# A three-branch decoder layer on one core: late loads behind casts, a split first cast, half of the cross scaling on GpSimd, and new places for the side work

## Chip, cores and metric

The kernel runs on one core of a Trainium2 chip. The time is device microseconds of one execution. The unchanged kernel takes 323.5 us (median of three runs, 323.2 to 323.61). The rows below come from one profiled execution that took 324.77 us, 1.27 us more than that median. TensorE was granted its upper level of 2.4 GHz throughout (mean granted clock 0.999 of full speed).

## What is computed

One decoder layer for 256 tokens of width 1024 in fp32. All shapes are those of the code; `rmsnorm`, `rope` and the two attentions' softmax are the usual ones.

```python
h = rmsnorm(x, g_in)
z = h @ w_in                                    # 1024 x 8776
(mq, mk, mv, mg, dq, dk, dv, dg, iq, ik, iw, xq, xg, glog) = jnp.split(z, offs, axis=-1)
ya = moba_attention(rope(mq), rope(mk), mv)     # 8 heads of 64, causal, one block of 256
ya = (ya * silu(mg)) @ w_up_moba
yb = dsa_attention(rope(dq), rope(dk), dv, rope(iq), rope(ik), iw)   # causal, top 64 keys
yb = (yb * silu(dg)) @ w_up_dsa
kv = rmsnorm(mem, g_mem) @ w_mem_kv             # 256 memory rows
xk, xv = kv[..., :512], kv[..., 512:]
yc = cross_attention(xq, xk, xv)                # 4 heads of 128
yc = (yc * silu(xg)) @ w_up_cross
gates = sigmoid(glog + b_merge)                 # 3 branches x 1024
u = gates[0] * ya + gates[1] * yb + gates[2] * yc
out = rmsnorm(x + u @ w_out, g_final)
```

## The kernel before

**Products.** An fp32 product is made of three matmuls in the type fp32r. Each operand is split into a high half (a cast to fp32r) and a low half (the operand minus its high half); high times high, high times low and low times high are added up in PSUM. The weights come from HBM in 100 pieces of up to 512 KB, called steps (w0, w1, ...). For each step the program loads the piece into a raw buffer (`load_weights`; four raw buffers, tag `wraw`), splits it (`split_weights`: ScalarE, ACT in the profile, writes the high half `w3h`, VectorE, DVE, the low half `w3l`), and TensorE multiplies. Loads are called six steps ahead (`LOAD_AHEAD`), the split three steps ahead (`SPLIT_AHEAD`). The pieces of steps 0 to 3 are cast in two parts. The first eight steps belong to mv and mq in turn (mv, mq, mv, mq, ...); then `ORDER` lists the blocks: `i0`, `dq0` and so on are column blocks of `w_in`, `xk0`, `xk1`, `xv` of `w_mem_kv`, `l10` is a block of the gate logits (branch 1, columns 256 times 0), `u00` a block of an up projection.

**Side work.** Everything else is hung on a step or half a step with `at(step, fn, ...)`, and the places stand in tables by hand: `M_PAIRS` and `D_PAIRS` (scores, transposes and values of the two self attentions), `X_HEADS` (the four cross heads: scores at h0, scaling at h0 + 0.5, transposes at h0 + 2, values at h0 + 3.5), `TURNS` (rope), `IDX` (the index heads of the sparse attention), `GATES` (silu), `MEM` (the four loads of the memory rows and their statistics). What a `w_in` block leaves in PSUM is evacuated at its end; for a logit block, `logit_evac` multiplies on DVE and then takes a Sigmoid on ACT.

**Order.** TensorE (PE) and GpSimd (POOL) run in the order of the program text. The rows of ACT, DVE and SyncE (SP), which issues most loads, are ordered by a scheduler, so a new place can move their rows as well. PE waits where an operand's half has not been written yet, or where a PSUM bank has not been read yet.

**The start.** The loads of x's first block and of steps 0 to 2 are issued on SP. `load_late` is called behind the cast of step 0: it issues step 3's weights and x's third pair of blocks on ACT (behind the last cast of w0), and steps 4 and 5 and x's last pair on SP. x in rows (`x_rows`, 1 MB, from which the norm is taken) is issued at step -2, and read by `xjunk` on ACT.

**The cross scaling.** In `cross_scale` DVE takes the reciprocal of the row sums (`xst`), and then ACT scales both halves of the head's probabilities (`xpr`, two of 128x256). The transposes (`xpt`) on PE read both. `self_scale` does the same for the self attentions, with both parts on POOL.

## Time and profile before

| | before |
|---|---|
| median of three runs | 323.5 us (323.2 to 323.61) |
| the profiled execution | 324.77 us |
| its span in the trace | 323.0 us |
| PE busy | 313.0 us (97%) |
| DVE busy | 252.1 us (78%) |
| ACT busy | 202.9 us (63%) |
| POOL busy | 41.9 us (13%) |
| chain that ended last | PE 70%, DVE 15%, DMA 5%, ACT 4%, issue 4% |

The span is the time from the first to the last instruction in the trace; the execution's own time has 1.77 us around it. The chain is followed back from the last instruction to whatever released each step of it. Rows of waits name the instruction that waited, what released it, and for how long.

### The profile page before, as it was taken

Reading aid. Unit: us, or ns where it says so; the run is one execution under the profiler, and the core shown is the slowest. Engines: PE = TensorE matmul, PEld = TensorE weight load, DVE = VectorE, ACT = ScalarE, POOL = GpSimd, SP = SyncE. Lnnn points to the kernel's source line nnn. Section 1 sums busy time; section 2 is a strip of 40 time slices with the busy share of each in tenths; the row PEclk is TensorE's granted clock in tenths of the full one; section 3 lists DMA queues with packets and bytes.
Section 4 is the critical chain, followed back from the end, with each engine's and each line's share of the span. In section 5 each row is a group of like instructions: output and inputs, shape, how many; then the busy total and the mean of one; then the engine's idle time right before and its main releaser. Section 6 shows DMA issues by size and latency. Waiting matters only on the chain.

```text
span 323.0 us, 6395 instructions
## 1 busy us (share of the span) xinstructions
PE 313.0 (97%) x2442; PEld 297.4 (92%) x2442; DVE 252.1 (78%) x458; ACT 202.9 (63%) x357; POOL 41.9 (13%) x58
## 2 busy tenths in 40 slices
PE   8899999998999999999999999999999999999992
PEld 7699999988999989879999999999999999998882
DVE  3579999899799999988766759998466775677523
ACT  5599674687878545577666588756444546643434
POOL 0001000017202000010200235321000111014011
PEclk9999999999999999999999999999999999999999
DMA  6989886864644446574443434478765666655003
GB/s 202 379 293 333 269 269 194 265 240 124 214 130 127 138 130 210 182 246 131 146 132 117 146 94 162 136 220 302 211 193 189 190 188 205 182 156 188 2 0 130
DMA packets 18368, 59.45 MB, mean 184 GB/s; under 512 B 2209, under 2 KB 2465, under 8 KB 18337
## 3 DMA queue, kind: packets, MB, share of 16 engines
q1 hardware_dynamic: 17760, 57.73, 57.1%
q10 hardware_dynamic: 576, 1.31, 1.0%
q8 instruction: 19, 0.31, 0.5%
q14 instruction: 13, 0.10, 0.1%
HBM read 55.89 MB, written 1.05 MB: 176 GB/s over the span
## 4 chain that ended last, share of the span: by engine, by line
PE 70%; DVE 15%; DMA 5%; ACT 4%; issue 4%; SPq 0%; ACTq 0%; DVEq 0%
DMA w3r<-w_in 3%; DVE wk L498 2%; DMA w25r<-w_in 2%; DVE m L496 1%; PE o_0ps L255 1%; PE o_0ps L256 1%; PE o_0ps L254 1%; DMA w0r<-w_in 1%; PE dya L642 1%; PE i_0ps L280 1%; PE i_1ps L280 1%; PE mv_1ps L280 1%; PE mv_0ps L280 1%; DVE acc L487 1%; PE lg L480 1%
## 5 line engine op out<-in xcount | busy, mean ns | idle before, releaser
L747 POOL TENSOR_TENSOR u<-u,gt 128x512 f32<-128x512 f32 x7 | 9.9, 1411 | 76.7 <-DVE gt L744 76.7
L616 POOL TENSOR_SCALAR dpr<-dpr,dst 128x128 f32<-128x128 f32 (+1 forms) x16 | 6.6, 425 | 84.1 <-DVE dst L614 83.9
L616 POOL TENSOR_SCALAR mpr<-mpr,mst 128x128 f32<-128x128 f32 (+1 forms) x16 | 9.8, 629 | 56.3 <-DVE mst L614 56.3
L734 ACT ACTIVATE gt<-gt,x_first 128x256 f32<-128x256 f32 x24 | 10.9, 501 | 2.7 <-DVE gt L731 2.5
L606 ACT ACTIVATE dpr<-dms,dst 128x128 f32<-128x128 f32 (+1 forms) x16 | 7.1, 446 | 3.6 <-DVE dst L602 3.6
L788 ACT ACTIVATE junk<-xn 128x512 f32<-128x512 f32 (+1 forms) x5 | 2.7, 543 | 8.6 <-DVE xn L786 8.6
L606 ACT ACTIVATE mpr<-mms,mst 128x128 f32<-128x128 f32 (+1 forms) x16 | 7.1, 444 | 1.2 <-DVE mst L602 1.2
L664 ACT ACTIVATE xpr<-xsc,xst,xs_rstd 128x256 f32<-128x256 f32 x8 | 4.4, 560 | 3.4 <-DVE xst L660 3.4
L752 ACT CAST us<-u 128x512 fp32r<-128x512 f32 x4 | 2.5, 624 | 6.2 <-POOL u L747 4.9
L647 ACT COPY dyT<-dya 64x256 f32<-64x256 f32 x8 | 2.9, 367 | 4.2 <-PE dya L642 4.1
L484 ACT ACTIVATE rl<-lg 128x384 f32<-128x384 f32 x8 | 3.9, 485 | 2.7 <-PE lg L480 1.6
L487 DVE SCALAR_TENSOR_TENSOR acc<-rl,iw,acc 128x128 f32<-128x128 f32 (+1 forms) x14 | 5.4, 431 | 0.1
L480 PE MATMUL lg<-ikT,iqT 128*128 128x128 f32 (+1 forms) x32 | 5.1, 282 | 0.1
L968 PE MATMUL warm<-ones 128*128 128x128 f32 x18 | 4.0, 419 | 1.1 <-DVE eps_t L963 1.1
L602 DVE CUSTOM_DVE_ANT_0 mms<-msc,bias_c 128x128 f32<-128x128 f32 (+1 forms) x16 | 5.0, 350 | 0.0
L968 PEld LDWEIGHTS warm<-ones 128*128 128x128 f32 x18 | 3.9, 328 | 1.1 <-DVE eps_t L963 1.1
L648 DVE TENSOR_TENSOR dyT<-dyT,dya 64x256 f32<-64x256 f32 x8 | 3.3, 417 | 1.8 <-ACT dyT L647 1.7
L628 ACT CAST dph<-dtp 128x384 fp32r<-128x384 f32 x8 | 3.8, 479 | 1.4 <-PE dtp L627 1.3
L629 DVE TENSOR_TENSOR dpl<-dtp,dph 128x384 fp32r<-128x384 f32 x8 | 4.4, 553 | 0.4
L602 DVE CUSTOM_DVE_ANT_0 dms<-dsc,sel 128x128 f32<-128x128 f32 (+1 forms) x16 | 4.7, 352 | 0.0
L786 DVE TENSOR_TENSOR xn<-o_0ps,xn 128x512 f32<-128x512 f32 x2 | 1.4, 691 | 4.2 <-PE o_0ps L256 4.2
L498 DVE MATCH_REPLACE8 wk<-m,wk 128x128 f32<-128x128 f32 (+1 forms) x14 | 4.7, 342 | 0.0
(1296 smaller groups left out, 1541.9 us busy)
## 6 DMA issues: line engine op xcount, KB each, us to landing
x_rows<-x SPq DMA_DIRECT2D x2, 512.0 KB, 8.7
eT<-memT SPq DMA_DIRECT2D x4, 256.0 KB, 4.6
xn<-x SPq DMA_DIRECT2D x2, 512.0 KB, 5.5
w0r<-w_in SPq DMA_DIRECT2D x2, 256.0 KB, 3.3
w1r<-w_in SPq DMA_DIRECT2D x2, 256.0 KB, 4.9
xT<-xT SPq DMA_DIRECT2D x2, 256.0 KB, 7.1
w2r<-w_in SPq DMA_DIRECT2D x1, 512.0 KB, 7.3
w3r<-w_in ACTq DMA_DIRECT2D x1, 512.0 KB, 8.7
```

The source lines that it names most:

```text
L280: nc.tensor.matmul(accs[nm][t][:, :n], a[p](k, slice(t * P, (t + 1) * P)), w[q][:, half, :], start=k + i == 0, stop=k + i == nk + 1,)
L480: nc.tensor.matmul(lg[:, c : c + n], q[:, q0:q1], idx["k"][:, j, 0:n], start=j == 0, stop=j == 1)
L487: nc.vector.scalar_tensor_tensor(acc[:, c], rl[:, c], iw[:, t, g : g + 1], (bias_c if g == 0 else acc)[:, c], op0=OP.mult, op1=OP.add,)
L498: nc.vector.match_replace(out=wk[:, c], in_to_replace=m8[t], in_values=src[:, c], imm_value=TAKEN)
L602: nc.vector.tensor_tensor_reduce(out=ms[:, c], in0=sc[:, c], in1=bias()[:, c], op0=OP.add, op1=OP.min, scale=-(HD**-0.5), scalar=3e38, acc ...
L606: big["last_exp"] = nc.scalar.activation(pr[:, c], ms[:, c], AF.Exp, bias=st[:, t : t + 1], scale=-1.0, accum_out=st[:, 2 + t : 3 + t],)
L616: nc.gpsimd.tensor_scalar(pr[:, c], pr[:, c], st[:, 4 + t : 5 + t], 1.0, op0=OP.mult, op1=OP.mult)
L629: nc.vector.tensor_sub(pl, tp[:, 0 : 3 * P], ph.bitcast(F32))
L664: big["last_exp"] = nc.scalar.activation(pr3[:, t, :], sc[:, t, :], AF.Exp, bias=st[:, t : t + 1], scale=xs_rstd[:, t : t + 1], accum_out= ...
L734: nc.scalar.activation(gt[:, f, :], gt[:, f, :], AF.Sigmoid, bias=x_first[:, j : j + 1])
L747: adder.tensor_tensor(u, u, gt, op=OP.add)
L968: nc.tensor.matmul(warm[:, 0:P], ones, ones, start=True, stop=True)
```

## The change

The order of the loads changes. x's third pair and step 3's weights are issued on ACT behind the first part of w1's cast (before: behind w0's cast), step 4's weights on ACT behind its second part (before: on SP); step 5's weights come before x's last pair on SP. `LOAD_ROWS` goes from -2 to 1, so `x_rows` is issued behind step 6's weights, and the constants behind `x_rows`. The first cast (128x512 of w0) is split by columns: ACT casts one half and DVE the other. In `cross_scale` POOL scales the second half of each head's probabilities. `ORDER` puts `xk1` ahead of `dv`, `l10` ahead of `dg0` (before: behind `xg1`), and changes the order of the last logit and up blocks; the place tables have new numbers.

```diff
@@ -62,24 +62,24 @@
 WARM = 9
 HALVED = 2
 ORDER = (
-    "mk0", "mk1", "i0", "dq0", "xq0", "i1", "dq1", "dk0", "dk1", "xk0", "xq1", "dv", "xk1",
-    "xv", "mg0", "mg1", "dg0", "dg1", "xg0", "xg1", "l10", "l01", "l00", "u00", "l02", "u10",
-    "l20", "l03", "u01", "u02", "l21", "u03", "u20", "l11", "u11", "l22", "l23", "u21", "l12",
+    "mk0", "mk1", "i0", "dq0", "xq0", "i1", "dq1", "dk0", "dk1", "xk0", "xq1", "xk1", "dv",
+    "xv", "mg0", "mg1", "l10", "dg0", "dg1", "xg0", "xg1", "l00", "u00", "l01", "l02", "u01",
+    "u10", "l03", "l20", "l21", "u20", "l11", "l23", "u03", "l22", "u11", "u02", "u21", "l12",
     "l13", "u12", "u13", "u23", "u22",
 )
-LOAD_ROWS = -2
+LOAD_ROWS = 1
 X_STATS = 6
 
-IDX = (27, 29, 33.5)
-
-TURNS = (('mq', 8.5, 15.5), ('mk', 13.5, 20.5), ('dq', 27, 30), ('dk', 34, 37.5))
-
-M_PAIRS = ((23, 25.5), (24, 27.5), (26.5, 29.5), (29.5, 31.5))
-D_PAIRS = ((43.5, 47.5), (47.5, 49), (52, 53.5), (54.5, 55.5))
-X_HEADS = (41.5, 44.5, 49, 50.5)
-GATES = 59.5
-
-MEM = (2, 7, 11, 15, 21.5)
+IDX = (27, 29, 34)
+
+TURNS = (('mq', 8.5, 15), ('mk', 14.5, 20.5), ('dq', 27, 33.5), ('dk', 36, 39))
+
+M_PAIRS = ((23, 25.5), (24.5, 27.5), (26.5, 29.5), (29.5, 31.5))
+D_PAIRS = ((43.5, 47.5), (47, 49), (52, 53.5), (54.5, 55.5))
+X_HEADS = (41.5, 44.5, 49, 50)
+GATES = 57.5
+
+MEM = (3, 7.5, 10.5, 13, 22)
 
 
 def block_places(blocks, nk):
@@ -224,7 +224,7 @@
 
 
     loaded, halves = {}, {}
-    last_hi = [None]
+    last_hi, last_load = [None], [None]
 
     def load_weights(s, j=None, queue=nc.sync):
         src, off, nk_all, n, k0, nk = plan.steps[s][0]
@@ -235,7 +235,9 @@
             tensor=src.tensor, offset=src.offset + off + (k0 + a) * n,
             ap=[[nk_all * n, P], [1, (b - a) * n]],
         )
-        queue.dma_start(loaded[s][:, a:b, :].rearrange("p k n -> p (k n)"), v)
+        last_load[0] = queue.dma_start(
+            loaded[s][:, a:b, :].rearrange("p k n -> p (k n)"), v
+        ).ins
 
     def split_weights(s):
         raw = loaded.pop(s)
@@ -245,7 +247,13 @@
         part = 1 if s < HALVED + 2 else shape[1]
         for j in range(0, shape[1], part):
             ks = slice(j, j + part)
-            last_hi[0] = nc.scalar.copy(hi[:, ks, :], raw[:, ks, :]).ins
+            cols = slice(0, shape[2] // 2 if s + j == 0 else shape[2])
+            last_hi[0] = nc.scalar.copy(hi[:, ks, cols], raw[:, ks, cols]).ins
+            if s + j == 0:
+                cols = slice(shape[2] // 2, shape[2])
+                nc.vector.tensor_copy(hi[:, ks, cols], raw[:, ks, cols])
+            if s == 1:
+                load_late(j)
             nc.vector.tensor_sub(lo[:, ks, :], raw[:, ks, :], hi[:, ks, :].bitcast(F32))
         halves[s] = (hi, lo)
 
@@ -609,13 +617,14 @@
                 )
             prs[nm, hd] = (pr, st)
 
+    def pool_scale(r, factor):
+        nc.gpsimd.tensor_scalar(r, r, factor, 1.0, op0=OP.mult, op1=OP.mult)
+
     def self_scale(nm, hd):
         pr, st = prs[nm, hd]
         nc.vector.reciprocal(st[:, 4:6], st[:, 2:4])
         for t, c in PARTS:
-            nc.gpsimd.tensor_scalar(
-                pr[:, c], pr[:, c], st[:, 4 + t : 5 + t], 1.0, op0=OP.mult, op1=OP.mult
-            )
+            pool_scale(pr[:, c], st[:, 4 + t : 5 + t])
 
     def self_transpose(nm, hd):
         pr, _ = prs.pop((nm, hd))
@@ -670,10 +679,8 @@
     def cross_scale(hd):
         pr, st = prs["x", hd]
         nc.vector.reciprocal(st[:, 4:6], st[:, 2:4])
-        for t in range(2):
-            nc.scalar.activation(
-                pr[:, t, :], pr[:, t, :], AF.Copy, scale=st[:, 4 + t : 5 + t]
-            )
+        nc.scalar.activation(pr[:, 0, :], pr[:, 0, :], AF.Copy, scale=st[:, 4:5])
+        pool_scale(pr[:, 1, :], st[:, 5:6])
 
     def cross_transpose(hd):
         pr, _ = prs["x", hd]
@@ -882,13 +889,14 @@
     attend("m", M_PAIRS, lambda: bias_c)
     attend("d", D_PAIRS, lambda: idx["sel"])
 
-    x_rows = []
+    x_rows, rows_load = [], [None]
 
     def load_rows():
         for t in range(2):
             rows = keep.tile([P, 4, S], F32, name=f"x_rows{t}", tag=("khi", "klo")[t])
             rows = rows.rearrange("p a b -> p (a b)")
-            nc.sync.dma_start(rows, x[t * P : (t + 1) * P, :])
+            with tc.issue_after(last_load[0]):
+                rows_load[0] = nc.sync.dma_start(rows, x[t * P : (t + 1) * P, :]).ins
             x_rows.append(rows)
 
     def start_stats():
@@ -959,6 +967,7 @@
     at(end["u01"], load_tail)
 
 
+    first = [load_act(xT, 0, "x", 0)]
     nc.vector.memset(ones, 1.0)
     nc.vector.memset(eps_t, EPS)
     nc.scalar.copy(ss[:, 3:4], eps_t)
@@ -966,36 +975,37 @@
     warm = psum.tile([P, 512], F32, name="warm", tag="tp", bufs=1)
     for _ in range(WARM):
         nc.tensor.matmul(warm[:, 0:P], ones, ones, start=True, stop=True)
-    first = [load_act(xT, 0, "x", 0)]
     load_weights(1, 0)
     load_weights(1, 1)
     first.append(load_act(xT, 0, "x", 1))
     load_weights(2)
 
-    def load_late():
+    def load_late(j):
 
         with tc.issue_after(last_hi[0]):
-            load_weights(3, queue=nc.scalar)
-            first.append(load_act(xT, 0, "x", 2, nc.scalar))
-        load_weights(4)
-        load_weights(5)
-        first.append(load_act(xT, 0, "x", 3))
+            if j == 0:
+                first.append(load_act(xT, 0, "x", 2, nc.scalar))
+                load_weights(3, queue=nc.scalar)
+            else:
+                load_weights(4, queue=nc.scalar)
+                load_weights(5)
+                with tc.issue_after(last_load[0]):
+                    first.append(load_act(xT, 0, "x", 3))
 
     for s in range(-SPLIT_AHEAD, n):
         p, rest = divmod(s + SPLIT_AHEAD, 2)
         if p < 4 and not rest:
             first[p]()
         if s == 4:
-            nc.sync.dma_start(cst, consts[:, 0:512])
-            nc.sync.dma_start(tabT.rearrange("p t c -> p (t c)"), consts[:, 512:1024])
+            with tc.issue_after(rows_load[0]):
+                nc.sync.dma_start(cst, consts[:, 0:512])
+                nc.sync.dma_start(tabT.rearrange("p t c -> p (t c)"), consts[:, 512:1024])
         for fn, args in plan.side.pop(s, []):
             fn(*args)
         if LOAD_AHEAD <= s + LOAD_AHEAD < n:
             load_weights(s + LOAD_AHEAD)
         if s + SPLIT_AHEAD < n:
             split_weights(s + SPLIT_AHEAD)
-            if s + SPLIT_AHEAD == 0:
-                load_late()
         if s >= 0:
             w = halves.pop(s)
             plan.steps[s][1](w, 0)
```

How rows move. First ACT, at the start of the program: the casts of w0 to w2 (`w0h`, ...), the casts of x's blocks (`xhi`) and the loads that ACT issues. Before:

```order
L248 CAST w0h<-w0r 128x512
L185 ACTIVATE xhi<-xT,x_first 128x256
L248 CAST w0h<-w0r 128x512
L177 DMA xT<-xT 128x512
L238 DMA w3r<-w_in 128x1024
L248 CAST w1h<-w1r 128x512 x2
L185 ACTIVATE xhi<-xT,x_first 128x256 x2
L248 CAST w2h<-w2r 128x512 x2
```

Now:

```order
L251 CAST w0h<-w0r 128x256
L185 ACTIVATE xhi<-xT,x_first 128x256
L251 CAST w0h<-w0r 128x512
L251 CAST w1h<-w1r 128x512
L177 DMA xT<-xT 128x512
L238 DMA w3r<-w_in 128x1024
L251 CAST w1h<-w1r 128x512
L238 DMA w4r<-w_in 128x1024
L185 ACTIVATE xhi<-xT,x_first 128x256 x2
L251 CAST w2h<-w2r 128x512 x2
```

The two loads stand one cast later, and a third one, w4's, has come in between the second cast of w1 and x's cast.

Second DVE, around step 20, where it evacuates the first cross query block (`xqT`) and turns the keys of the first attention (`mkT`). Before:

```order
L249 TENSOR_TENSOR w22l<-w22r,w22h 128x640
L249 TENSOR_TENSOR w23l<-w23r,w23h 128x640
L562 TENSOR_TENSOR xqT<-xq0ps,xqT 128x512
L532 TENSOR_TENSOR mkT<-mkT,mksw 128x1024
L249 TENSOR_TENSOR w24l<-w24r,w24h 128x1024
```

Now:

```order
L257 TENSOR_TENSOR w22l<-w22r,w22h 128x640
L570 TENSOR_TENSOR xqT<-xq0ps,xqT 128x512
L257 TENSOR_TENSOR w23l<-w23r,w23h 128x640
L540 TENSOR_TENSOR mkT<-mkT,mksw 128x1024
L257 TENSOR_TENSOR w24l<-w24r,w24h 128x1024
```

The subtraction of step 23's weights has moved from ahead of `xqT` to behind it.

Third ACT, at steps 50 to 52, between the transposes of the sparse attention (`dph`) and the next cast of its probabilities (`dpr`), where the last cross head is handled (`xpr`). Before:

```order
L628 CAST dph_2296<-dtp_2298 128x384
L664 ACTIVATE xpr_2335,xst_2332<-xsc_2325,xst_2332,xs_rstd 128x256 x2
L248 CAST w55h<-w55r 128x1024
L647 COPY dyT<-dya_2289 64x256
L688 CAST xph_2361<-xpt_2356 128x512
L674 ACTIVATE xpr_2335<-xpr_2335,xst_2332 128x256 x2
L248 CAST w56h<-w56r 128x1024
L606 ACTIVATE dpr_2414,dst_2413<-dms_2412,dst_2413 128x128
```

Now:

```order
L637 CAST dph_2297<-dtp_2299 128x384
L741 ACT_TABLE_LOAD
L741 ACTIVATE gt_2318<-gt_2318,x_first 128x256 x2
L673 ACT_TABLE_LOAD
L673 ACTIVATE xpr_2315,xst_2312<-xsc_2305,xst_2312,xs_rstd 128x256 x2
L656 COPY dyT<-dya_2290 64x256
L695 CAST xph_2367<-xpt_2362 128x512
L682 ACTIVATE xpr_2315<-xpr_2315,xst_2312 128x256
L251 CAST w55h<-w55r 128x1024
L251 CAST w56h<-w56r 128x1024
L695 CAST xph_2434<-xpt_2429 128x512
L614 ACTIVATE dpr_2417,dst_2416<-dms_2415,dst_2416 128x128
```

The two Sigmoids of `l10` (`gt`) now stand between two groups of exponentials, each time with a load of ACT's function table ahead of the next function, and `xpr` is scaled once here instead of twice.

## Rows read from the trace of the kernel before

**Rows 1.** The page's chain that ended last, by engine.

```profile
PE 70%; DVE 15%; DMA 5%; ACT 4%; issue 4%; SPq 0%; ACTq 0%; DVEq 0%
```

**Rows 2.** PE timeline, first matmuls of steps 2, 4 and 6; columns: start us, us, engine, line.

```profile
11.99 0.50 PE L280 MATMUL mv_0ps<-w2h,xhi 128*128 128x512 f32 x1 [0.34 <-ACT w2h L248]
...
18.86 0.40 PE L280 MATMUL mv_0ps<-w4h,xhi 128*128 128x512 f32 x1
...
24.45 0.40 PE L280 MATMUL mv_0ps<-w6h,xhi 128*128 128x512 f32 x1
```

**Rows 3.** ACT timeline at the start; in brackets the idle time before and its releaser.

```profile
5.62 0.39 ACTq L177 DMA_DIRECT2D xT<-xT  x1
6.05 1.31 ACTq L238 DMA_DIRECT2D w3r<-w_in  x1
7.41 0.62 ACT L248 CAST w1h<-w1r 128x512 fp32r<-128x512 f32 x1 [1.17 <-DMA w1r<-w_in]
8.57 0.62 ACT L248 CAST w1h<-w1r 128x512 fp32r<-128x512 f32 x1 [0.54 <-DMA w1r<-w_in]
9.83 0.91 ACT L185 ACTIVATE xhi<-xT,x_first 128x256 fp32r<-128x256 f32 x2 [0.64 <-DMA xT<-xT]
11.32 1.14 ACT L248 CAST w2h<-w2r 128x512 fp32r<-128x512 f32 x2 [0.58 <-DMA w2r<-w_in]
14.76 1.14 ACT L248 CAST w3h<-w3r 128x512 fp32r<-128x512 f32 x2 [2.30 <-DMA w3r<-w_in]
```

**Rows 4.** What the DMA engines moved in 0 to 25 us, 40 slices.

```profile
GB/s 0 0 23 234 242 288 311 256 285 229 292 236 246 252 311 262 374 390 416 410 403 416 420 429 413 426 419 420 419 367 380 321 157 177 167 49 292 331 308 387
```

**Rows 5.** PE's weight-load waits, 22 to 200 us: total, times, longest.

```profile
PEld mya L642 <- DVE mpl L629: 1.2, 1, 1.2
PEld xpt L684 <- ACT xpr L674: 0.7, 2, 0.5
```

**Rows 6.** DVE timeline, 57 to 64 us.

```profile
57.94 0.81 DVE L249 TENSOR_TENSOR w23l<-w23r,w23h 128x640 fp32r<-128x640 f32 x1
59.33 0.69 DVE L562 TENSOR_TENSOR xqT<-xq0ps,xqT 128x512 fp32r<-128x512 f32 x1 [0.58 <-ACT xqT L561]
...
63.81 0.17 DVE L219 RECIPROCAL m_rstd<-en 128x2 f32<-128x2 f32 x1 [0.32 <-ACT en L218]
```

**Rows 7.** DVE and POOL timeline, 76 to 78 us, and POOL's scalings by form, 140 to 200 us.

```profile
76.33 1.20 DVE L249 TENSOR_TENSOR w29l<-w29r,w29h 128x1024 fp32r<-128x1024 f32 x1
76.41 1.47 POOL L616 TENSOR_SCALAR mpr<-mpr,mst 128x256 f32<-128x256 f32 x1
...
L616 POOL TENSOR_SCALAR dpr<-dpr,dst 128x256 f32<-128x256 f32 x8 | 3.8, 479 | 0.0
```

**Rows 8.** Timeline of all engines at the first cross head's scaling.

```profile
140.91 0.16 DVE L672 RECIPROCAL xst<-xst 128x2 f32<-128x2 f32 x1
...
140.99 1.23 DVE L249 TENSOR_TENSOR w47l<-w47r,w47h 128x1024 fp32r<-128x1024 f32 x1
...
141.10 0.91 ACT L674 ACTIVATE xpr<-xpr,xst 128x256 f32<-128x256 f32 x2
```

**Rows 9.** Timeline of all engines, 171 to 182 us.

```profile
171.64 0.56 ACT L664 ACTIVATE xpr<-xsc,xst,xs_rstd 128x256 f32<-128x256 f32 x1 [1.48 <-DVE xst L660]
...
176.55 1.23 DVE L249 TENSOR_TENSOR w56l<-w56r,w56h 128x1024 fp32r<-128x1024 f32 x1 [0.34 <-ACT w56h L248]
...
177.69 0.28 DVE L602 CUSTOM_DVE_ANT_0 dms<-dsc,sel 128x128 f32<-128x128 f32 x1
...
179.37 1.70 POOL L616 TENSOR_SCALAR dpr<-dpr,dst 128x128 f32<-128x128 f32 x4 [18.98 <-DVE dst L614]
...
181.31 0.27 PE L627 MATMUL dtp<-cst,dpr 128*128 128x128 f32 x1
```

**Rows 10.** ACT timeline at a load of the function table, 190 us.

```profile
190.29 1.28 ACT L720 ACT_TABLE_LOAD   x1
...
191.58 0.63 ACT L720 ACTIVATE mgsg<-mgzn 128x512 f32<-128x512 f32 x1
```

## The prediction

> **What bounds the kernel now.** I read the chain that ended last first, since it shows which engine sets the end: PE has most of it, DVE the largest share of the rest, DMA comes third [rows 1]. So time can only come from places where PE waits, and I looked for those in PE's timeline and its waits. There are three kinds. At the start PE waits for the halves of w1 to w3, and these wait for loads [rows 2, 3]. From 22 to 200 us the two largest waits are one of 1.2 us for a low half on DVE (`mpl`) and one of 0.7 us for the scaled cross probabilities (`xpr`) [rows 5]. From 200 us on there is nothing of this size, and I found none that the new order of the last blocks would make. The third view is DVE's timeline: from 60 to 141 us it is nearly without gaps, and both of those waits are waits for DVE, the second by way of the reciprocal ahead of the scaling. In that stretch DVE sets when PE goes on, and a gain at the start is worth what DVE gets of it.
>
> **The start.** Steps 4 and 5, in which PE hardly waits, take 5.59 us, 2.80 each (18.86 to 24.45); steps 2 and 3 take 6.87 (11.99 to 18.86) [rows 2]. ACT shows why: the cast of w2 waits for its load until 11.32, that of w3 stands idle for 2.30 us until 14.76, and the first cast of w1 begins only at 7.41, when the issue of w3's load (6.05 + 1.31 = 7.36) is over [rows 3].
>
> I walk ACT through its new order. Without the two loads ahead of it w1's first cast can begin at about 7.0 (its data is there by then, as ACT is held by the issue and not by the load). The two loads are issued while that cast runs, as they were beside w0's second cast: 0.39 + 1.31 us end at 8.8. w1's second cast starts there instead of at 8.57, and ends at 9.4. If w4's issue costs 0.4 us it lies under that cast; if it costs 1.3 as w3's did, ACT is held until 10.15. Then x's casts (0.91) and the first of w2 (0.62) follow: w2's first high half is written at 11.0 or at 11.7, and was at 11.94.
>
> Can the data be there? Up to 10 us, slices 1 to 16 of the DMA row sum to 2.17 MB [rows 4]. What must have landed by w2 is 2.07 MB (x's first block and its constants, 148 KB; w0 and w1, 512 KB each; x's second block, 128 KB; x's second pair, 256 KB; w2, 512 KB); before, w3, w4, x's other pairs and the first half of `x_rows` shared the engines with it. At the same rates w2 lands near 10.2 by that count. x's third pair and w3 are 0.77 MB more, at some 0.25 MB a 0.625 us slice, so w3 lands near 12.5, and near 13 with some of w4 and w5 in between. Both are estimates from [rows 4]. They leave PE held by the casts alone at step 2, and by nothing at step 3: step 2 starts at 11.35 (PE has first to finish step 1), lasts 3.15 with the wait for its first low half as before, step 3 takes 2.8, and step 4 starts at 17.3 instead of 18.86. I take -1.5 us. The bounds are -0.1 (loads land as late as before; the rest of the order is no worse) and -1.8 (all issues at 0.4). Splitting the first cast brings the first matmul forward by some 0.2 us, but step 1 then waits for w1, so I count nothing for it.
>
> **From there to 141 us.** PE runs on unhindered to `xqT`, where DVE has waited 0.58 us for PE's result [rows 6], so DVE is earlier there by the whole 1.5. Now w23's subtraction stands behind `xqT` instead of ahead of it, and costs the 0.74 us by which one such row follows another (it filled time there that nobody needed). Of that 0.32 comes back, the gap ahead of `m_rstd` [rows 6], which then is covered. So DVE keeps 1.5 - 0.74 + 0.32 = 1.1 us; I say +0.42 for this term, between 0 and +0.74. Behind it the same DVE work stands ahead of the first cross head as before, in another order (`mpl` ahead of w29's subtraction, the index evacuation ahead of w27's). The wait of 1.2 us at `mya` becomes shorter, but PE then reaches the next transposes earlier, and these need a bank that DVE reads at the end of the same work: what is saved at one is waited at the other. 0, from -0.3 to +0.3.
>
> **The cross scaling.** For the first head PE waits for ACT's two scalings, which end at 142.01 [rows 8]. POOL takes 0.48 us for such a half when it runs alone, but 1.47 when it starts beside a subtraction of two SBUF operands: its row begins at 76.41 and ends at 77.88, 0.35 us after w29's subtraction (77.53) [rows 7]. For the first head exactly such a subtraction, w47's, starts at 140.99, straight behind the reciprocal that POOL waits for [rows 8], and ends at 142.22. POOL's half would be ready at 142.22 + 0.35 = 142.57 instead of 142.01: +0.56. Should POOL be first, it would be ready near 141.9, and the gain would be 0.1 to 0.3. I take the blocked case, since both the order of DVE's rows and their times put the subtraction first. At the other heads the reciprocal is followed by an instruction with an operand in PSUM, or PE comes later than the result; 0.
>
> The Trainium skill has a rule for this (SBUF — State Buffer, "Who interferes with whom"): a DVE instruction with two SBUF inputs and a GpSimd instruction that reads SBUF exclude each other, and the one that issues second is held for the whole of the other. The row of 76.41 agrees with it.
>
> **The Sigmoids of l10.** They now stand between exponentials, so ACT loads its function table twice more, at 1.28 us each; the next instruction follows at once [rows 10]. With the two Sigmoids (0.91, as two ACT rows of this size take in [rows 8]) this is 3.47 us ahead of the last cross head's exponentials. ACT has been idle there for 1.48 us [rows 9], and saves 0.46 twice, once on each of the two scalings of the third and fourth head: 3.47 - 1.48 - 0.92 = 1.07 us late. DVE's w56l waits for ACT, and `dms` stands behind it at 177.69; so the next probabilities are late by 1.07. POOL's first two scalings for them end at 180.2 (half of the 1.70 that begin at 179.37), and PE's transposes `dtp` read them at 181.31 [rows 9]: a margin of 1.1 us, all of it used. I count +0.2, between 0 and +1.
>
> By the Trainium skill (ScalarE: Activation LUTs, "What ACT_TABLE_LOAD costs") each change of the table also costs a drain of 1.38 us, 2.66 us in all; by it the sum would be 2.8 us larger, 326.0 us. The trace shows no drain: 190.29 + 1.28 = 191.57, and the Sigmoid starts at 191.58.
>
> **The sum.** -1.5 + 0.42 + 0.56 + 0.2 = -0.32. The profiled execution is 324.77, so 324.45; it lies 1.27 above the median of the runs, so 323.2 us. Less than 0.2% (0.65 us) is about what a measurement here cannot tell from no change; this is inside.
>
> **The rivals.**
> - *Faster, 322.3 us.* POOL comes first at the first head, or is not held (-0.1 in place of +0.56), and the tables are covered: -1.5 + 0.42 - 0.1 = -1.2. For it: the gap between reciprocal and subtraction is a few hundredths of a microsecond, and a small shift of w47's cast on ACT, which the subtraction needs, turns the order round. Against it: at 76.41 the scaling met such a subtraction 0.08 us after its start, as it would here, and took 1.47.
> - *Slower, 324.5 us.* The loads behind the casts gain nothing: each issue on ACT takes 1.3 us, or w3 lands no earlier because the memory's path is as full as before. Then DVE is not ahead at `xqT` (-0.1 + 0.42), and POOL's block and the tables stay, +0.56 and +0.2: +1.1. It decides from about w3's cast at 14 us on. For it: the only load of 512 KB issued on ACT took 1.31 us, and two are issued there now. Against it: over 1 MB (w4, x's last pair, the first half of `x_rows`) no longer shares the way with w2 and w3.
> - *The gain at the start is lost whole.* DVE falls back to its old place between 60 and 141 us, as its work is what counts there: 0 + 0.56 + 0.2 = +0.8, 324.2 us. For it: DVE's rows there have hardly a gap. Against it: DVE itself waits for PE at `xqT`.
> - *POOL is held at more heads than the first* (at the third, w54's subtraction follows its reciprocal): another 0.56 for each of up to two heads, 323.8 to 324.3.
> - *A change of the table stops ACT for longer than its row.* The margin at `dtp` is used up already, so all of it is PE's; were it as much again as the row for both loads, 2 x 1.28 = 2.6, 325.8 us. Against it: the Sigmoid at 191.58 follows its table at once [rows 10].
>
> **Chances.** My forecast (POOL held, start gained) 0.40; the faster rival 0.35; no gain by the loads 0.09; gain lost whole 0.08; more heads held 0.06; longer tables 0.02. My own case spreads by its bounds over 322.4 to 323.9: 0.08 of its 0.40 fall below 322.85. Of the faster rival 0.06 stay within 0.2% (with a poor start), and of the held heads 0.03. So faster 0.35 - 0.06 + 0.08 = 0.37, same 0.40 - 0.08 + 0.06 + 0.03 = 0.41, slower 0.09 + 0.08 + 0.03 + 0.02 = 0.22. A tenth left out at either end gives 322.0 to 324.3.
>
> **What would show it.** Step 4 should start near 17.3, w3's cast without a wait, w1's first cast near 7.0. w23's subtraction should stand behind `xqT` and DVE be about 1 us earlier at `m_rstd`. `xpr`'s POOL row of the first head should take 1.4 us or more and end after ACT's half, with PE's wait at `xpt` near 1.2 us in place of 0.7. Two table loads near 170 us, and a short wait at `dtp` near 181. I am wrong if ACT's issues hold the casts, if POOL's half takes 0.48, if PE waits at `dtp` for over half a microsecond, or if new waits come up behind 200 us.

## The result and the profile after

The change made the kernel slower. The changed kernel takes 325.52 us (median of four runs, 325.17 to 325.76), the kernel before 323.35 us on the same chip (four runs, 323.08 to 323.61). The ratio is 1.0066, with a 95% interval of 1.0049 to 1.0084. That is about 2.2 us more, where the prediction was 323.2 us and its range ended at 324.3. The profiled execution took 325.73 us, with a span of 323.9 us: 0.96 us more than the profiled execution of before (324.77). Three executions of the runs below took 383.6, 511.8 and 1574.2 us; they are left out of every median, spread and ratio.

The chain that ended last, by engine, answers to [rows 1]:

```profile
PE 72%; DVE 9%; ACT 8%; DMA 5%; issue 3%; SPq 1%; POOL 0%; ACTq 0%; DVEq 0%; POOLq 0%
```

DVE's share fell from 15% to 9% and ACT's rose from 4% to 8%: some waits have passed from DVE to ACT. PE's largest waits from 22 to 200 us, as its weight loads (PEld) show them, answer to [rows 5]. `mq_0ps` is the product of step 7, `xpt` the transposes of a cross head, `iqt` and `ikt` the transposes for the index of the sparse attention, `mya` the values of the first attention:

```profile
PEld mq_0ps L264 <- DVE w7l L257: 1.1, 1, 1.1
PEld xpt L691 <- ACT xpr L682: 1.0, 2, 0.6
PEld xpt L691 <- POOL xpr L621: 0.8, 1, 0.8
PEld iqt L461 <- DVE mst L610: 0.7, 2, 0.6
...
PEld ikt L465 <- DVE mpl L638: 0.4, 1, 0.4
...
PEld mya L651 <- DVE mpl L638: 0.3, 1, 0.3
PEld mq_0ps L262 <- ACT w7h L251: 0.3, 1, 0.3
...
```

The old wait at `mya` (1.2 us) is down to 0.3, but several waits have come up beside it, the largest of them at step 7, where the prediction had none.

PE's timeline, with the first matmul of steps 4, 7, 30, 44 and 58, and the gap inside step 7:

```profile
17.37 0.39 PE L288 MATMUL mv_0ps<-w4h,xhi 128*128 128x512 f32 x1
...
25.81 0.39 PE L262 MATMUL mq_0ps<-xhi,w7h 128*128 128x256 f32 x1
26.04 0.28 PE L263 MATMUL mq_0ps<-xlo,w7h 128*128 128x256 f32 x1
27.20 0.38 PE L264 MATMUL mq_0ps<-xhi,w7l 128*128 128x256 f32 x1 [0.88 <-DVE w7l L257]
...
96.29 0.28 PE L262 MATMUL xk_0ps<-ehi,w30h 128*128 128x256 f32 x1
...
143.88 0.28 PE L262 MATMUL mg0ps<-xhi,w44h 128*128 128x256 f32 x1
...
200.14 0.28 PE L262 MATMUL l00ps<-xhi,w58h 128*128 128x256 f32 x1
```

The same places in the kernel before:

```profile
96.75 0.28 PE L254 MATMUL xk_0ps<-ehi,w30h 128*128 128x256 f32 x1
...
143.85 0.28 PE L254 MATMUL mg0ps<-xhi,w44h 128*128 128x256 f32 x1
...
199.15 0.28 PE L254 MATMUL l01ps<-xhi,w58h 128*128 128x256 f32 x1
```

Step 4 comes 1.49 us earlier (18.86 in [rows 2]), step 30 only 0.46, step 44 no longer earlier at all (0.03 later), step 58 0.99 later. Up to step 58 both kernels have done the same blocks. So the gain is there at the start, shrinks twice, and the loss arises between 140 and 200 us. From step 58 on nothing is added.

### The profile page after: what moved, and what is told of

Its sections match the earlier page's. It is cut to its first block, busy times and chain, and to the rows that moved or that the text cites. A ratio compares the mean times of both kernels' runs of the same rounds, so it can differ in the third digit from the quotient of the medians.

```text
span 323.9 us, 6396 instructions
## 1 busy us (share of the span) xinstructions
PE 313.6 (97%) x2442; PEld 297.9 (92%) x2442; DVE 249.5 (77%) x459; ACT 204.1 (63%) x355; POOL 46.6 (14%) x62
## 3 DMA queue, kind: packets, MB, share of 16 engines
HBM read 55.89 MB, written 1.05 MB: 176 GB/s over the span
## 4 chain that ended last, share of the span: by engine, by line
PE 72%; DVE 9%; ACT 8%; DMA 5%; issue 3%; SPq 1%; POOL 0%; ACTq 0%; DVEq 0%; POOLq 0%
DMA w8r<-w_in 2%; DMA w3r<-w_in 2%; PE dv_0ps L288 2%; PE xv_0ps L288 2%; PE xv_1ps L288 2%; PE dv_1ps L288 2%; DMA w1r<-w_in 1%; PE lg L488 1%; PE o_0ps L263 1%; PE o_0ps L264 1%; PE o_0ps L262 1%; DVE mms L610 1%; PE i_0ps L288 1%; PE i_1ps L288 1%; PE o_1ps L264 1%
## 5 line engine op out<-in xcount | busy, mean ns | idle before, releaser
L621 POOL TENSOR_SCALAR mpr<-mpr,mst 128x128 f32<-128x128 f32 (+1 forms) x16 | 8.9, 572 | 57.7 <-DVE mst L625 57.6
L621 POOL TENSOR_SCALAR xpr<-xpr,xst 128x256 f32<-128x256 f32 x4 | 2.7, 677 | 60.5 <-DVE xst L681 60.5
L621 POOL TENSOR_SCALAR dpr<-dpr,dst 128x128 f32<-128x128 f32 (+1 forms) x16 | 7.7, 493 | 21.2 <-DVE dst L625 21.1
L760 DVE TENSOR_TENSOR us<-u,us 128x512 fp32r<-128x512 f32 x4 | 2.7, 686 | 4.2 <-ACT us L759 4.2
L915 POOL COPY bias_c<-cst 128x128 f32<-128x128 f32 x1 | 1.3, 1281 | 26.2 <-DMA cst<-consts 26.2
L799 POOL TENSOR_TENSOR xn<-xn,gf 128x512 f32<-128x512 f32 x2 | 2.6, 1292 | 15.9 <-ACT junk L795 15.9
```

The lines of the kernel that those rows point to most:

```text
L621: nc.gpsimd.tensor_scalar(r, r, factor, 1.0, op0=OP.mult, op1=OP.mult)
```

## The experiments

All times in us; the median of before is from the same chip. Each median is of 6 to 12 executions, that of before of 23 to 26. The ratio is not the quotient of the two medians (0.9990 for before_again, 1.0039 for start_only), so a difference of 0.1% between two rows says little. The last two columns are from the profiled execution: PE's time from the start of step 30 to that of step 44, and from there to step 58.

| run | median | before | ratio (interval) | profiled, span | step 30 to 44 | step 44 to 58 |
|---|---|---|---|---|---|---|
| before | | | | 324.77, 323.0 | 47.10 | 55.30 |
| changed kernel | 325.52 | 323.35 | 1.0066 (1.0049 to 1.0084) | 325.73, 323.9 | 47.59 | 56.26 |
| start_only | 325.33 | 324.07 | 1.0065 (1.0036 to 1.0094) | 328.37, 326.6 | 47.08 | 55.36 |
| all_but_start | 325.62 | 324.07 | 1.0054 (1.0036 to 1.0072) | 325.52, 323.7 | 47.60 | 56.25 |
| all_but_pool | 328.36 | 324.07 | 1.0140 (1.0112 to 1.0167) | 329.11, 327.3 | 47.09 | 60.20 |
| before_again | 323.75 | 324.07 | 1.0002 (0.9988 to 1.0017) | 324.6, 322.8 | 47.08 | 55.30 |
| no_l10 | 324.73 | 324.0 | 1.0020 (1.0005 to 1.0035) | 324.08, 322.3 | 47.63 | 55.70 |
| pool_only | 324.45 | 324.0 | 1.0012 (0.9999 to 1.0026) | 325.06, 323.2 | 47.65 | 55.31 |
| places_only | 325.32 | 324.0 | 1.0039 (1.0021 to 1.0057) | 324.35, 322.6 | 47.11 | 56.10 |
| rows_early | 327.14 | 324.0 | 1.0102 (1.0068 to 1.0137) | 325.18, 323.4 | 47.63 | 56.27 |
| after_again | 325.05 | 323.78 | 1.0044 (1.0029 to 1.0058) | 325.05, 323.3 | 47.62 | 56.24 |
| l10_only | 324.87 | 323.78 | 1.0039 (1.0022 to 1.0056) | 325.42, 323.6 | 47.10 | 56.39 |
| head3_late | 325.86 | 323.78 | 1.0075 (1.0056 to 1.0094) | 325.88, 324.1 | 47.62 | 56.95 |
| no_l10_act | 324.73 | 323.78 | 1.0023 (1.0004 to 1.0041) | 324.04, 322.3 | 47.10 | 56.11 |
| early_only | 324.31 | 323.7 | 1.0008 (0.9988 to 1.0028) | 323.93, 322.1 | 47.10 | 55.36 |
| tables_only | 324.85 | 323.7 | 1.0027 (1.0007 to 1.0047) | 324.94, 323.1 | 47.09 | 56.09 |
| early_start | 323.72 | 323.49 | 1.0011 (0.9993 to 1.0030) | 323.43, 321.6 | 47.07 | 55.35 |
| head3_back | 323.99 | 323.49 | 1.0020 (1.0004 to 1.0037) | 324.45, 322.7 | 47.08 | 55.62 |
| before_look2 | | | | 324.68, 322.9 | 47.11 | 55.31 |
| places_look2 | | | | 324.93, 323.1 | 47.09 | 56.09 |

Behind step 30 the profiles of one program agree within 0.04 us. POOL's half adds 0.5 us from step 30 to 44 (47.59 to 47.65 in the seven profiles that have it, 47.07 to 47.11 in the others), and l10 with the later places adds 0.9 us from step 44 to 58 (56.24 to 56.27 in the four profiles that have all of these places and POOL's half, 55.30 to 55.36 in the seven that have none). Ahead of step 30 they do not agree: step 8 starts at 29.47, 30.19 and 30.35 in the three profiles of before, at 30.02 and 29.17 in the two of the changed kernel.

### The loads at the start

**start_only**: the kernel before with the new loads at the start and nothing else of the change.

```diff
-LOAD_ROWS = -2
+LOAD_ROWS = 1
...
+            if s == 1:
+                load_late(j)
```

> The kernel before with the new start alone (late loads, split first cast, x in rows behind w6, constants behind it). Theory A: the usual start of before is nearly as good, and the wait for w7's halves at step 7 (1.35 us in the changed kernel) is a pure loss: 0.9 to 1.4 us slower than before, near 324.5. Rival B: 1.5 gained at the start and 1.35 lost at step 7, within 0.3 us of before.

**all_but_start**: the changed kernel with the old loads at the start.

```diff
-LOAD_ROWS = 1
+LOAD_ROWS = -2
...
-            if s == 1:
-                load_late(j)
```

> The changed kernel with the start of before (the order of blocks, the places and the half of the cross scaling on GpSimd stay). Theory A: what is left is the waits at the cross transposes and at dtp (0.5 + 0.55 + 0.25, less 0.3 gained between 60 and 96 us): about 1.0 us slower than before, near 324.4. Rival B: all of the loss is left, about 2.1 us slower, near 325.5.

**before_again**: the kernel before once more. **before_look2**: a third profile of it, one execution.

> The kernel before once more, for a second profile of it. Theory A (the profiled execution that the prediction was worked from had an untypically slow start, as it lay 1.3 us above the median): step 4 starts near 17.5 us instead of 18.86, the issue of w3's load on ACT takes about 0.45 us instead of 1.31, and the span is near 321.7 us. Rival B (that start is the usual one): step 4 again near 18.9, issue 1.3, span near 323.

> The kernel before, a third profile. Theory A: the waits at the start and at mBt and mya vary with when the loads land, by 1 to 2 us together between executions, and nothing behind 100 us varies. Rival B: all executions wait alike, and the difference between a profiled and a typical time lies outside the span.

all_but_start loses about as much as the whole change (1.0054), and its trace loses the same behind step 30, so the loss does not lie in the loads. start_only (1.0065) was expected to be 0.9 to 1.4 us slower, or level. Its profile holds a wait of 1.8 us at `mBt` (the transposes of the memory rows' norm factor, `m_rstd`, which DVE writes) and a stretch at half the clock (last section), and its runs spread from 324.2 to 328.8; it says little about the loads. before_again has step 4 at 18.06 with the same program and step 30 at 96.60 against 96.75: with the old places, most of a gain of 0.8 us at the start was gone by step 30, 0.6 of it as larger waits at `mBt` (1.1 for 0.7) and `mya` (1.4 for 1.2). before_look2 shows the same from the other side: step 4 at 19.01, step 30 at 96.63.

**rows_early**: the changed kernel with x in rows loaded earlier, to take away the wait at step 7.

```diff
-LOAD_ROWS = 1
+LOAD_ROWS = -1
```

> The changed kernel with x in rows issued behind step 5's weights instead of behind step 6's. Theory A (the start's gain is lost at step 7, where w7's cast stands behind the second xjunk, which waits for x in rows): PE's wait of 1.35 us at step 7 goes, and 0.4 to 1.3 us of it reach the end, as DVE's chain at 60 to 96 us takes part of it. Rival B (DVE's chain sets the time from 60 us on): the wait at step 7 goes, and PE waits as much longer at mBt, mya, iqt and ikt; the time stays.

In its trace the wait at step 7 is gone: the second `xjunk` starts at 19.53 without idle time (22.16 in the changed kernel) and w7's cast at 23.04 (24.73). The DVE-bound waits grow (`iqt` 0.9 for 0.7, `mya` 0.5 for 0.3), and of the 1.05 us that step 8 gains 0.6 are left at step 30. Its time got worse, 1.0102: its runs lie between 325.18 and 329.51 us, and the profiled one is the lowest of them, so the trace does not show what the others lost. That stays open.

### The places and the Sigmoids of l10

**places_only**: the kernel before with the new `ORDER`, but `l10` left behind `xg1`, and with all the new tables. **places_look2**: a second profile of the same kernel, one execution.

```diff
-    "xv", "mg0", "mg1", "l10", "dg0", "dg1", "xg0", "xg1", "l00", "u00", "l01", "l02", "u01",
+    "xv", "mg0", "mg1", "dg0", "dg1", "xg0", "xg1", "l10", "l00", "u00", "l01", "l02", "u01",
```

(shown against the changed kernel's `ORDER`)

> The kernel before with the new places and the new order of blocks, but l10 behind xg1, the start of before and the scaling on ACT. Theory A (the places shorten PE's waits between 60 and 100 us by 0.5 us and nothing else changes): 0.15% faster than before, near 0.9985. Rival B (DVE's chain takes it back): no difference.

> The new places with the new order of blocks and l10 behind xg1, a second profile (the first was the fastest of its nine executions). Theory A (waits for loads in the first 70 us vary): PE's waits ahead of 70 us are 0.5 to 1.5 us larger than in the first profile, and those behind 100 us are the same. Rival B: the profile is like the first, and the slower runs differ in something behind 100 us.

places_only was expected to gain 0.15% or nothing and lost 0.39%. Its two profiles differ by 0.6 us at step 30 (95.55 and 96.15), 0.5 of it at `mBt` (0.7 and 1.2), and by nothing behind it.

**tables_only**: the kernel before with all the new tables and the old `ORDER`. **early_only**: of these only the tables that act ahead of step 43 (index, ropes, first attention, memory rows).

```diff
-IDX = (27, 29, 33.5)
+IDX = (27, 29, 34)
...
-MEM = (2, 7, 11, 15, 21.5)
+MEM = (3, 7.5, 10.5, 13, 22)
```

(two of the tables that both runs change)

> The kernel before with all new places and the old order of blocks. Theory A (the later places cost it: the fourth cross head at 50 meets ACT's scaling too early, 0.6 us near 175 us in the profile of the new places): 0.1 to 0.2% slower than before. Rival B (the order of blocks costs it): no difference from before, or faster.

> The kernel before with the new places ahead of step 43 alone (index heads, ropes, first attention, loads and statistics of the memory rows); order of blocks, later places, start and scaling as before. Theory A (the early places shift PE's waits among mBt, mya, lg and iqt and shorten them by 0.5 us together): 0.1 to 0.2% faster than before. Rival B (they are what makes the new places slower, by loads that stand behind the memory rows and rope copies on SP's queue): 0.3% slower or more, with ACT waiting for weights between 40 and 60 us.

The early places cost and gain nothing that can be measured (1.0008); all the tables together cost 0.27%. The two intervals overlap, so the times alone do not settle what the later places cost. The traces do: from step 44 to 58 tables_only takes 0.73 us more than early_only (56.09 and 55.36), and 0.7 of it is one wait. At the fourth cross head, half a step earlier than before, PE's transposes now come ahead of DVE. The waits of tables_only:

```profile
PEld xpt L684 <- ACT xpr L674: 0.7, 2, 0.5
PEld mBt L913 <- PE i_1ps L280: 0.7, 1, 0.7
PEld lg L480 <- DVE mst L602: 0.7, 1, 0.7
PEld xpt L684 <- DVE xpl L689: 0.7, 1, 0.7
```

The fourth is new: the transposes of the fourth head wait until DVE has read the third head's bank. early_only doesn't have it.

**l10_only**: the kernel before with `l10` ahead of `dg0`. **no_l10**: the changed kernel with `l10` back behind `xg1` (the diff of places_only).

```diff
-    "xv", "mg0", "mg1", "dg0", "dg1", "xg0", "xg1", "l10", "l01", "l00", "u00", "l02", "u10",
+    "xv", "mg0", "mg1", "l10", "dg0", "dg1", "xg0", "xg1", "l01", "l00", "u00", "l02", "u10",
```

> The kernel before with l10 ahead of dg0 as the only edit (start, places and scaling as before). Theory A (the two more table loads and the Sigmoids between the exponentials cost PE its waits at the last cross head and at dtp): with the fourth head's scores half a step later and ACT scaling both halves, PE waits 0.5 to 1.5 us more between 170 and 185 us; 0.2 to 0.4% slower. Rival B (they only fill ACT's idle time): within 0.1%.

> The changed kernel with the gate logit block l10 back behind xg1, so that no Sigmoid stands between exponentials; all else as changed. Theory A (the table loads hold ACT, and so the fourth head's transposes and dtp): PE's waits of 0.55 at xpt near 176 us and 0.25 at dtp near 182 us go, about 0.9 us faster than the changed kernel, that is about 0.2% slower than before. Rival B (GpSimd's half holds these): the waits stay, and the time with them.

l10 alone costs 0.39%, about 1.3 us, and 1.1 us in the trace (56.39 for 55.30 from step 44 to 58). The first three waits of its trace hold the place that the prediction named, `dtp`, with 1.1 us where the prediction counted 0.2:

```profile
PEld mya L642 <- DVE mpl L629: 1.2, 1, 1.2
PEld dtp L627 <- POOL dpr L616: 1.1, 1, 1.1
PEld xpt L684 <- ACT xpr L674: 0.7, 2, 0.5
```

Without l10's new place the changed kernel's ratio falls to 1.0020, and step 44 to 58 takes 55.70 us instead of 56.26. So l10 costs 1.1 us by itself and 0.6 on top of the other places: it is a large part of the loss, but the other places without it (places_only) lost 0.39% as well.

**head3_late**: the changed kernel with the fourth head back at 50.5. **head3_back**: the same edit without l10's new place and with ACT alone scaling (no_l10_act, below).

```diff
-X_HEADS = (41.5, 44.5, 49, 50)
+X_HEADS = (41.5, 44.5, 49, 50.5)
```

> The changed kernel with the fourth cross head at 50.5 instead of 50, as before. Theory A (its transposes wait 0.55 us because ACT scales the first half behind the two table loads): half a step later PE meets them 1.4 us later and does not wait; 0.5 us faster than the changed kernel, that is 0.45 to 0.5% above before. Rival B (the wait only moves on to dtp): the wait at dtp grows by as much, and the time stays.

> The changed kernel with l10 behind xg1, the fourth cross head at 50.5 and both halves of the scaling on ACT: start, the other places and the order of the last blocks are new. Theory A: without the three named waits (0.5 + 0.9 us) it is 0.8 us faster than the changed kernel by these and as fast as before or up to 0.3% faster. Rival B: still 0.2% slower than before, so that something else in the start or the places costs it.

In head3_late the fourth head's wait at `xpt` is gone, and the wait at `dtp` is 1.3 us instead of 0.3; the time is not better (1.0075), and step 44 to 58 takes 0.7 us longer (56.95). The two places share one delay: ACT and DVE are late by the tables, and PE pays for it at whichever comes first. With l10 out of the way the head's place counts for 0.5 us in the trace (55.62 in head3_back, 56.11 in no_l10_act), which the times do not show (1.0020 and 1.0023). head3_back is still 0.2% slower than before, so the fourth head's place is not all that is left.

### GpSimd's half

**pool_only**: the kernel before with POOL scaling the second half. **no_l10_act**: no_l10 with ACT scaling both. **all_but_pool**: the changed kernel with ACT scaling both. The edit of the last two, which pool_only makes the other way round:

```diff
-        nc.scalar.activation(pr[:, 0, :], pr[:, 0, :], AF.Copy, scale=st[:, 4:5])
-        pool_scale(pr[:, 1, :], st[:, 5:6])
+        for t in range(2):
+            nc.scalar.activation(
+                pr[:, t, :], pr[:, t, :], AF.Copy, scale=st[:, 4 + t : 5 + t]
+            )
```

> The kernel before with half of the cross scaling on GpSimd alone. Theory A (GpSimd's half is held by w47's subtraction at the first head and nowhere else): PE's second wait at the first head's transposes grows from 0.34 to about 0.9, 0.5 us slower than before (0.15%). Rival B (ACT's saved time is worth more): within 0.1% or faster.

> The changed kernel with l10 back behind xg1 and both halves of the cross scaling on ACT: start and places alone are new. Theory A (GpSimd's half costs 0.5 us at the first head): 0.4 us faster than with l10 back alone, so 0.05 to 0.1% above before. Rival B (ACT's saved time pays for it): as slow as that or slower, 0.2% above before.

> The changed kernel with both halves of the cross scaling on ACT again. Both theories: the waits of PE at the first and fourth head's transposes shrink by about 1.0 us together (0.5 and 0.5), so about 324.5, and ACT's scaling for the fourth head comes 0.46 us later. If the waits at the transposes come from the table loads and not from POOL, the time stays near 325.3.

pool_only shows the wait of 0.8 us at `xpt` for POOL, 0.5 us more from step 30 to 44, and costs 0.12% (0.4 us), with an interval that just reaches no change. no_l10_act and no_l10 do not differ in time, although the first has the 0.8 us wait no more: its fourth head waits 0.7 for DVE instead of 0.3, and step 44 to 58 takes 0.4 us longer. all_but_pool is no test of POOL: the scheduler placed ACT's rows otherwise and put exponentials between l10's two Sigmoids, so that ACT loads its table four times, at 169.95, 171.76, 174.27 and 179.78 us, and PE waits 3.2 us at the fourth head. What it does show is the price of four such loads close together: 5.1 us of ACT, and step 44 to 58 takes 4.9 us longer than before.

### What is left over

**after_again**: the changed kernel once more. **early_start**: the early places together with the new loads.

```diff
+    first = [load_act(xT, 0, "x", 0)]
...
+            if s == 1:
+                load_late(j)
```

(on top of early_only)

> The changed kernel once more, for a second profile of it. Theory A (what the second half of x in rows takes to land decides the wait at step 7: 8.5 us in the first profile gave 1.35 us of wait, 7.0 us gave none where l10 was put back): the waits at xpt near 176 us (0.55) and dtp near 182 us (0.25) are there again, the one at step 7 may be or not, and the time is 0.4 to 0.7% above before either way. Rival B (the step 7 wait is a fixed part of the new start): it is there again at 1.0 us or more.

> The kernel before with the new start and the new places ahead of step 43; order of blocks, later places and scaling on ACT as before. Theory A (the start gains 1.3 us of PE's waits and loses up to 1.0 at step 7 when x in rows lands late; nothing behind 100 us is touched): 0.3 to 1.0 us faster than before, ratio 0.997 to 0.999. Rival B (the new start costs time in typical executions by loads that land late): not faster, 1.000 to 1.003.

early_start has the shortest profiled execution of all (323.43 us; step 52 at 174.49, where early_only has 174.99 and before 175.85), and yet 1.0011 in time; early_only without the loads has 1.0008. So what the traces show of a gain by the early places and the loads, carried to step 52, cannot be found in the timed runs. No version was faster than the kernel before. The timed losses (by the ratio) are nearer to what the traces lose behind step 30 alone: 1.5 us for the whole change (timed 1.4 in after_again, 1.8 in all_but_start, 2.1 in the first runs), 1.1 for l10_only (1.3), 0.8 for tables_only (0.9), 0.6 for pool_only (0.4). places_only, rows_early and start_only lost 0.4 to 2.1 us more than that.

## Why the prediction was wrong

The prediction reckoned -0.32 us from one profiled execution to the other; 0.96 was measured. By the steps' starts above, -0.46 of it (of -1.08 that the prediction had) is there at step 30. From step 30 to 44 PE takes 47.59 us (47.10 before): +0.49, where the prediction had +0.56. From step 44 to 58 it takes 56.26 (55.30 before): +0.96, where the prediction had +0.2. None of the prediction's signs of being wrong came up: the issues did not hold the casts, POOL's half did not take 0.48, PE waited 0.3 at `dtp`, and nothing is added behind 200 us. Two of its rivals' sums are rounded down (324.6 and 324.3 by their terms); nothing hangs on it.

**The start: right in the mechanism, the size right in this pair of traces (17.37 where 17.3 was reckoned).** ACT's timeline answers to [rows 3]:

```profile
6.84 0.62 ACT L251 CAST w1h<-w1r 128x512 fp32r<-128x512 f32 x1 [0.50 <-DMA w1r<-w_in]
6.85 0.39 ACTq L177 DMA_DIRECT2D xT<-xT  x1
7.27 0.45 ACTq L238 DMA_DIRECT2D w3r<-w_in  x1
...
7.78 0.42 ACTq L238 DMA_DIRECT2D w4r<-w_in  x1
...
13.27 1.14 ACT L251 CAST w3h<-w3r 128x512 fp32r<-128x512 f32 x2 [1.52 <-DMA w3r<-w_in]
```

The issues took 0.45 and 0.42 us and not 1.31. w3's cast still waits 1.52 us for its load, against "without a wait", but it now ends before PE needs it. That the gain is 1.49 is in part the luck of which execution was profiled: against the other two profiles of before (step 4 at 18.06 and 19.01) the same start is worth 0.7 and 1.6.

**"PE runs on unhindered to `xqT`": the step that failed first.** The prediction counted the later `x_rows` (`LOAD_ROWS`) only as room for the loads ahead of it, and did not ask when its reader would get it. ACT, in order:

```profile
19.28 1.06 ACT L906 ACTIVATE xjunk<-x_rows 128x1024 f32<-128x1024 f32 x1 [0.16 <-DMA x_rows<-x]
...
22.16 1.06 ACT L906 ACTIVATE xjunk<-x_rows 128x1024 f32<-128x1024 f32 x1 [1.73 <-DMA x_rows<-x]
...
23.32 1.28 ACT L218 ACT_TABLE_LOAD   x1
...
24.73 1.03 ACT L251 CAST w7h<-w7r 128x1024 fp32r<-128x1024 f32 x1
```

ACT takes its rows in order. The cast of w7 stands behind the statistics of x, these wait 1.73 us for the second half of `x_rows`, and then comes a table load of 1.28; w7's high half is late for PE by 0.3 us, and its low half on DVE (25.92 + 1.23 = 27.15) by another 1.1. By how much depends on when `x_rows` lands: in after_again the second `xjunk` starts at 21.31 and the gap is 0.24 us, in rows_early there is none. Behind step 7 the rest went the predicted way: w23's subtraction stands behind `xqT`, `mya` waits less, and `iqt` and `ikt` wait instead.

**POOL at the first cross head: right.** Reckoned +0.56, and step 30 to 44 grew by 0.5, as it did in every run with POOL's half. The timeline answers to [rows 8]:

```profile
140.41 0.18 DVE L681 RECIPROCAL xst<-xst 128x2 f32<-128x2 f32 x1
140.48 1.23 DVE L257 TENSOR_TENSOR w47l<-w47r,w47h 128x1024 fp32r<-128x1024 f32 x1
140.63 0.51 ACT L682 ACTIVATE xpr<-xpr,xst 128x256 f32<-128x256 f32 x1 [0.61 <-DVE xst L681]
140.78 1.27 POOL L621 TENSOR_SCALAR xpr<-xpr,xst 128x256 f32<-128x256 f32 x1 [41.35 <-DVE xst L681]
...
142.11 0.55 PE L691 MATMUL xpt<-cst,xpr 128*128 128x128 f32 x3 [0.59 <-POOL xpr L621]
```

POOL's half begins 0.30 us after the subtraction and ends 0.34 after it; ACT's half had ended 0.91 earlier. At the fourth head, with no such subtraction beside it, the same row took 0.48 us. This is the rule of the Trainium skill that the prediction named (SBUF — State Buffer, "Who interferes with whom"), and the trace agrees: 1.27 against 0.48.

**The tables of l10: the right mechanism, +0.2 where +0.96 was measured.** Of the 0.96, 0.4 are there without l10 (no_l10: 55.70). ACT's and POOL's timelines answer to [rows 9]:

```profile
170.07 1.28 ACT L741 ACT_TABLE_LOAD   x1
171.36 0.91 ACT L741 ACTIVATE gt<-gt,x_first 128x256 f32<-128x256 f32 x2
172.28 1.28 ACT L673 ACT_TABLE_LOAD   x1
173.57 0.56 ACT L673 ACTIVATE xpr<-xsc,xst,xs_rstd 128x256 f32<-128x256 f32 x1
...
175.19 0.59 ACT L695 CAST xph<-xpt 128x512 fp32r<-128x512 f32 x1
175.67 0.51 ACT L682 ACTIVATE xpr<-xpr,xst 128x256 f32<-128x256 f32 x1
...
179.75 0.40 ACT L614 ACTIVATE dpr<-dms,dst 128x128 f32<-128x128 f32 x1 [1.20 <-DVE dst L610]
...
181.46 2.71 POOL L621 TENSOR_SCALAR dpr<-dpr,dst 128x128 f32<-128x128 f32 x4 [5.84 <-DVE dst L625]
```

The loads took just their rows (172.28 + 1.28 = 173.56, and the exponential starts at 173.57), so the rival with longer tables is out; nor is there the drain of 1.38 us per change that the Trainium skill has (ScalarE: Activation LUTs, "What ACT_TABLE_LOAD costs"). Two parts of the sum were wrong. Of the two savings of 0.46 the first was used up: the third head's scaling began 0.29 later than before (168.64 and 168.35), so `dph` ended at 170.05, 0.1 earlier and not 0.46. The fourth head's exponentials came 1.93 us later than before (173.57 and 171.64) and POOL's scaling of the next probabilities 2.09 later (181.46 and 179.37), where 1.07 was reckoned. And "at the other heads ... PE comes later than the result; 0" failed at the fourth: its place had moved from 50.5 to 50, its transposes come half a step earlier, and ACT's scaling, behind the tables, comes at 175.67. PE waits there first (0.6 us for ACT and 0.4 more for DVE to free the bank), and only 0.3 at `dtp`. l10_only and head3_late show the same delay paid at `dtp` (1.1 and 1.3 us). tables_only pays 0.7 at the fourth head without l10. What makes up the last 0.3 us, which head3_back still has (55.62), stays open.

**From the profile to the median: the step that failed by most in numbers.** The prediction took 1.27 us off its profiled time, as that of before lay above its median. The changed kernel's profiled execution lies only 0.21 above its own (325.73 and 325.52), that of after_again at its median (325.05 both). The three profiled executions of before lie 0.5 to 1.4 us above the medians of before on their chips. So 1.06 of the 2.3 us by which the prediction missed are this subtraction, and the other 1.3 are the terms above (0.6 at step 7 and behind it, -0.1 at the first head, 0.8 at l10's tables and the fourth head). What a typical execution of before does better than the profiled one stays open, since no trace of one was taken. It probably lies ahead of step 30, since behind it all profiles of before agree. That early_start gains over 1 us in its trace and nothing in time would fit it, and so would the timed losses, which are nearer to the waits behind step 30 alone: a typical execution of before may already have much of what the traces gain at the start, and then the term of -1.5 + 0.42 is the one that failed. This is argued and not shown.

Of the rivals, that the gain at the start is lost whole comes nearest (0 + 0.56 + 0.2, with l10's term at 0.96); that the issues on ACT would hold the casts was wrong.

## What to carry to other kernels

When an edit moves a transfer, look up every reader of it on an engine that runs in order, and what stands behind that reader: here the cast of w7, which the diff does not touch, waited for `x_rows`. A place moved earlier by half a step has to be checked against the engine that feeds it as the rest of the same change leaves it, since a margin that is used up at one place is paid at the next. And a gain in a stretch that differs from execution to execution (step 4 at 18.06, 18.86 and 19.01 with the same program) should not be counted in full against a median.

## What the runs showed of the hardware

**The granted clock after a wait of PE.** In start_only PE waited 1.61 us for `m_rstd` until 68.56, and the clock was granted at 0.50 of full speed (1.2 GHz) from 70 to 75 us, as the windows of the trace show (columns: stretch, busy time of PE, PEld, DVE, ACT, POOL, granted clock, DMA share, GB/s):

```profile
66.00:70.00 4.00, 2.39 (x12) 2.15 (x12) 3.71 (x16) 3.77 (x8) 0.00 (x0) 0.80 0.77 268
70.00:75.00 5.00, 5.00 (x28) 4.45 (x27) 4.98 (x20) 3.24 (x8) 1.36 (x4) 0.50 0.55 193
75.00:80.00 5.00, 5.00 (x44) 5.00 (x43) 2.99 (x12) 3.34 (x12) 1.82 (x4) 0.98 0.00 0
```

PE was busy throughout in both of the last two stretches, with 28 rows of matmuls in the one and 44 in the other (their shapes differ somewhat). From step 23 to 43 start_only took 76.68 us, before 73.31: 3.4 us more, of which PE's weight-load waits are 0.7 (3.5 and 2.8). In all_but_pool PE waited 3.06 us until 178.74, and the granted clock was 0.66 as a mean from 180 to 185 us; step 44 to 58 took 4.9 us more, of which its waits are 3.3 (3.9 and 0.6). So these two waits cost more than their length.

**The issue of a load on ACT is no fixed price.** At its old place the issue of w3's load took 0.52 to 1.31 us in the ten traces that have it there (0.61, 1.17 and 1.31 in the three of before); at the new one it took 0.45 us in all ten. What makes it long is not shown.
